# Weight splits moved from GpSimd to VectorE, and four numbers of the planner changed, in a hybrid attention layer

## The chip, the cores and the metric

One Trainium2 chip, one core. The metric is device microseconds of one execution; the time of a kernel is the median of its runs. Engines are named as in the profile: PE is TensorE (PEld its weight load, which overlaps it), DVE VectorE, ACT ScalarE, POOL GpSimd, SP the engine that issues most transfers.

## What is computed

One decoder layer on 2048 tokens of width 1024, float32:

```
h = rms_norm(x)
c_q, c_kv, k_rope, gdn_qkv, gdn_a, gdn_b, mem_q, gate = split(h @ w_in)
o_mla = causal softmax attention, 4 heads, q and k from low-rank c_q, c_kv, with rotary parts
o_gdn = gated delta rule in chunks, 4 heads:
    T = (strict_lower(k_beta k^T * decay) + I)^-1         # one triangular system per chunk
    v_new = u - w @ state;  o = q e^g @ state + a @ v_new  # state carried from chunk to chunk
o_mem = softmax attention over 256 memory tokens, 4 heads, k and v = rms_norm(mem) @ w_mem_kv
x = x + concat(o_mla, o_gdn, o_mem) * silu(gate) @ w_out
return rms_norm(x)
```

## The kernel before, in words

All large products run on PE in a float32 form of reduced width. To keep precision each operand is split into a high part (a rounded copy) and a low part (the rest), and a product is three matmuls: high by high, high by low, low by high (`mm3`).

Three stages follow each other. **The input projection** takes the tokens in two halves (`hf`) of two blocks of 512 tokens (`b`), and streams the columns of `w_in` as units: a unit is half the depth of 128 columns, one load `wr` of 256 KB, one split into `wh` (copy on ACT, sometimes DVE) and `wl` (subtraction, `w_split`, L614), and 24 matmuls `ip`. Beside it run the background jobs: the delta-rule heads (`delta_head`), the low-rank products (`low_rank`, with `q_use` and `kv_use`, matmuls `qb`, `kb`, `vb`) and the projection of the memory tokens (`mem_proj`, matmuls `mk` and `mv`); their weights are loaded as `bw` and split into `bwh` and `bwl` in `small_weights` (L1100). **Attention** has the matmuls `sc` (scores), `pt` (transposes of the probabilities) and `av` (values). **The output projection** has `op`.

For a delta-rule head, rows of decays and norms go to memory and come back broadcast over the partitions (`gr`, `fr`); there are two loads of `gr`, one for each block, and the second is issued after the first block's last product `kk` (L929). The triangular systems of a head are solved on POOL: the matrices go out (`lsys`), come in as `lt` (L944), 62 POOL instructions on `pr` and `X` solve them, the result goes out (`tsys`) and in (`inv`), and DVE transposes and PE matmuls `inv` build the larger inverse (L966 and below). The scan over the chunks (`pa`, `r`, `vn`, `st`) follows.

The order of the work is set by **a planner in the kernel's own Python**. It keeps a clock for each engine (`T`), adds a modelled cost for each instruction (`pool_cost` L223 for POOL, `pool_dma` L284 for its transfers), and after each group of PE work (`pump`) resumes the background jobs whose time has come: `yield n` in a job asks for at least n ns on PE's clock before its next step. The framework's scheduler may still move an instruction within its queue. Every operation is recorded at one line (L259), SP's transfers at L305, POOL's at L294. `lesser(name)` (L628) chooses POOL for a subtraction when the modelled POOL is free and no solve is near (`solving`), DVE otherwise.

A tile's buffer comes from a ring with a fixed number of places; a new tile waits until the instructions that read the old one in its place are done. `wr` has two places, so that the load of a unit waits for the `wl` of the unit two before it. Scores `s` and the solver's `lt` are in one ring (`page`).

Of the kernel before, what the change touches and what calls it, by code (L numbers as in the profile page):

```python
# [67 lines left out]
def hybrid_layer(ctx, tc, a, out):  # L68
# [84 lines left out]
    in_psum = set()  # L153
    tiles = set()
    step_end = [0.0]
    solving = [0.0]
    tab = [None]

    def free(ap):
        return int(np.prod(ap.shape[1:]))  # L160
# [61 lines left out]

    def pool_cost(op, args, kw, out):  # L223
        if op == "tensor_tensor":
            return 147 + 2.1 * free(out)
        fast = op == "tensor_scalar" and kw["op0"] == ALU.mult and kw.get("op1") == ALU.add
        return 160 + (0.85 if fast or op == "memset" else 3.4) * free(out)

# [55 lines left out]
    def pool_dma(out, in_):  # L284

        touch(in_, out)
        t = max(T["POOL"], T["PE"], arrival(in_, "POOL"), used.get(out.tensor.name, 0.0),
                floor.get(out.tensor.name, 0.0)) + 600
        T["POOL"] = t
        t += 1500 + free(out) * out.shape[0] * 4 / 200  # L290
        wrote(out, "SP", t + 1000)
        step_end[0] = max(step_end[0], t + 1000)
        used[in_.tensor.name] = max(used.get(in_.tensor.name, 0.0), t + 200)
        pinned(nc.gpsimd.dma_start(out=raw(out), in_=raw(in_)))  # L294
# [319 lines left out]
    def w_split(w):  # L614
        wh = sb.tile([P, 512], F32R, name="wh", tag="wh", bufs=3)
        copy(wh, w)
        wl = sb.tile([P, 512], F32R, name="wl", tag="wl", bufs=3)
        lesser("wl").tensor_tensor(wl, w, wh, op=ALU.subtract)
        return wh, wl

    def copy(out, in_):
# [5 lines left out]

    def lesser(name):  # L628

        return G if max(T["POOL"], solving[0]) <= T["PE"] + SLACK[name] else V  # L630

    class Job:

# [209 lines left out]
    def delta_head(hf, h, q, k, res):  # L843
# [52 lines left out]
        for b in range(2):  # L896
            bs = slice(b * 512, (b + 1) * 512)
            nq, nb, ne = (t.rearrange("p (c t) -> p c t", t=P) for t in cur)

            gc = cols[:, 0, h * 8 + b * 4:h * 8 + b * 4 + 4]  # L900
            gr3 = gr.rearrange("p (c t) -> p c t", t=P)
            V.tensor_tensor(gr3, gr3, gc.unsqueeze(2).broadcast_to([P, 4, P]), op=ALU.subtract)
            V.tensor_tensor(gr3, gr3, neg.unsqueeze(1).broadcast_to([P, 4, P]), op=ALU.add)
            A.activation(gr, gr, AF.Exp)
            k3, q3 = (t[:, bs].rearrange("p (c t) -> p c t", t=P) for t in (k, q))
            V.tensor_tensor(kq[:, :, 0, :], k3, nb, op=ALU.mult)
            yield 0
            V.tensor_tensor(kq[:, :, 1, :], q3, nq, op=ALU.mult)
            V.tensor_tensor(q3, q3, ne, op=ALU.mult)
            V.tensor_tensor(gr3, gr3, nk[:, b * 4:b * 4 + 4].unsqueeze(2).broadcast_to([P, 4, P]), op=ALU.mult)  # L910
            yield 0
            if b == 0:
                cur = rows(1)
                yield SPARE
            for c2 in range(2):
                ps = psg("kk")
                for c in range(2):
                    cc = c2 * 2 + c
                    PE.matmul(ps[:, c * 256:(c + 1) * 256], k[:, b * 512 + cc * P:b * 512 + (cc + 1) * P],
                              kq[:, cc, :, :], start=True, stop=True)  # L920
                o = b * 4 + c2 * 2
                ps4 = ps.rearrange("p (c i t) -> p c i t", c=2, i=2)
                dec = gr3[:, c2 * 2:c2 * 2 + 2, :]
                V.tensor_tensor(LT[:, o:o + 2, :], ps4[:, :, 0, :], dec, op=ALU.mult)
                atm = sb.tile([P, 2, P], F32, name="atm", tag="atm", bufs=2)
                V.tensor_tensor(atm, ps4[:, :, 1, :], dec, op=ALU.mult)
                dma(out=at_d[hf][h][:, o * P:(o + 2) * P], in_=atm.rearrange("p c t -> p (c t)"), awaited=False)
                if b == 0 and c2 == 1:
                    gr = decay_row(1)  # L929
                yield 0  # L930
        give(A=1)
        done["rows"] = done.get("rows", 0) + 1
        for bk in range(4):
# [8 lines left out]
        pool_dma(out=X, in_=a["eye4"])  # L942
        for cs in range(4):
            pool_dma(out=lt[cs * 32:(cs + 1) * 32].rearrange("p j i -> p (j i)"), in_=lsys[hf][h])  # L944
        solving[0] = T["POOL"] + 25000
        yield 2000
        pr = sb.tile([P, 80], F32, name="pr", tag="pr", bufs=1)
        for j in range(31):
# [5 lines left out]
            G.tensor_tensor(X[:, 0:n, j + 1:32], X[:, 0:n, j + 1:32], prv, op=ALU.subtract)  # L954
        for cs in range(4):
            pool_dma(out=tsys[hf][h].rearrange("s (n e) i -> e s n i", e=4)[cs], in_=X[cs * 32:(cs + 1) * 32])
        solving[0] = T["POOL"] + 12000
        yield from take(TT=1)
        yield 0
        give(lt=1)  # L960
# [8 lines left out]
        for n in (32, 64):  # L969
            pairs = [(2 * n * p, slice(2 * n * p, 2 * n * p + n), slice(2 * n * p + n, 2 * n * p + 2 * n))  # L970
                     for p in range(64 // n)]
            mid = t2("mid", (P, 8 * n))
            mid3 = mid.rearrange("p (c t) -> p c t", t=n)

            def sl(c):
                return slice(c * n, (c + 1) * n)
            for o, lo, hi in pairs:
                for i in range(n // 32):
                    for j in range(i, n // 32):
                        src, dst = slice(o + i * 32, o + i * 32 + 32), slice(o + j * 32, o + j * 32 + 32)  # L980
                        V.transpose(mid3[dst, :, i * 32:i * 32 + 32], TT[src, :, dst])
                        if i < j:
                            G.memset(mid3[src, :, j * 32:j * 32 + 32], 0.0)
            yield 0
            ps = psg("inv")
            for c in range(NCK):
                for o, lo, hi in pairs:
                    PE.matmul(ps[hi, sl(c)], LT[lo, c, hi], mid[lo, sl(c)], start=True, stop=True)
            for o, lo, hi in pairs:
                if o:  # L990
                    A.activation(mid[hi, :], ps[hi, 0:8 * n], AF.Copy, scale=-1.0)
                else:
                    V.tensor_scalar(mid[hi, :], ps[hi, 0:8 * n], -1.0, None, op0=ALU.mult)
            yield 0
            ps = psg("inv")
            for c in range(NCK):
                for o, lo, hi in pairs:
                    PE.matmul(ps[lo, sl(c)], mid[hi, sl(c)], TT[hi, c, hi], start=True, stop=True)
            for o, lo, hi in pairs:
                (A.copy if o else V.tensor_copy)(TT[lo, :, hi], ps[lo, 0:8 * n].rearrange("p (c t) -> p c t", t=n))  # L1000
            yield 0
# [89 lines left out]
    def small_weights(srcs):  # L1091
# [6 lines left out]
        def split(w):  # L1098
# [1 line left out]
            wh = sb.tile([P, n], F32R, name="bwh", tag="m2", bufs=9)  # L1100
            copy(wh, w)
            wl = sb.tile([P, n], F32R, name="bwl", tag="m2", bufs=9)
            lesser("bwl").tensor_tensor(wl, w, wh, op=ALU.subtract)
            return wh, wl
        w = load(srcs[0])
        yield 2800
# [50 lines left out]
    def q_use():  # L1157
# [9 lines left out]
        def use(hf, t, hs, ls, wh, wl):  # L1167
# [10 lines left out]
            for b in range(2):  # L1178
# [1 line left out]
                cs, sn = t2("cs"), t2("sn")  # L1180
                trig_load(cs, 0, hf * 2 + b, 4)
                trig_load(sn, 1, hf * 2 + b, 4)
                yield 2000
                r1, r2 = project(b, hs, ls, *half), project(b, hs, ls, wh, wl)
                tA, tB, tC = t2("ra"), t2("rb"), t2("rc")
                V.tensor_tensor(tA, r1, cs, op=ALU.mult)
# [1010 lines left out]
```

## Time and profile before

| what | us |
|---|---|
| median of 3 runs (1814.57 to 1819.68) | 1818.56 |
| the profiled execution, its own time | 1822.34 |
| its span on the core | 1820.6 |
| PE busy in the span | 1746.9 (96%) |
| DVE busy | 1158.6 (64%) |
| POOL busy | 500.4 (27%) |

The span is the time from the first to the last instruction on the core. Busy times overlap between engines. An engine's idle time is put down to what ended it. The granted clock of TensorE is 1.00 at 2.4 GHz and 0.50 at 1.2 GHz, so that a stretch's mean between these tells how much of it ran at the lower level. The projection ends near 1110 us, attention near 1550 us.

### The profile page before, as it was taken

Reading aid. Unit: us, or ns where it says so; the run is one execution under the profiler, and the core shown is the slowest. Engines: PE = TensorE matmul, PEld = TensorE weight load, DVE = VectorE, ACT = ScalarE, POOL = GpSimd, SP = SyncE. Lnnn points to the kernel's source line nnn. Section 1 sums busy time; section 2 is a strip of 40 time slices with the busy share of each in tenths; the row PEclk is TensorE's granted clock in tenths of the full one; section 3 lists DMA queues with packets and bytes.
Section 4 is the critical chain, followed back from the end, with each engine's and each line's share of the span. In section 5 each row is a group of like instructions: output and inputs, shape, how many; then the busy total and the mean of one; then the engine's idle time right before and its main releaser. Section 6 shows DMA issues by size and latency. Waiting matters only on the chain.

```text
span 1820.6 us, 28632 instructions
## 1 busy us (share of the span) xinstructions
PE 1746.9 (96%) x9776; PEld 1471.2 (81%) x9776; DVE 1158.6 (64%) x2622; ACT 734.6 (40%) x1884; POOL 500.4 (27%) x894
## 2 busy tenths in 40 slices
PE   7999999999999999899999997999999999999998
PEld 5778788888777777788888876899999998888886
DVE  6777766786785858445566653777676778345443
ACT  6444233342442535213453423455455556222121
POOL 1422752443521124352112625001111012412120
PEclk9999999999999999999999998999999999999999
DMA  7544474456555344564555479145252527566551
GB/s 265 163 128 150 137 237 137 131 160 211 154 170 176 121 147 116 184 194 138 182 199 176 141 216 265 61 127 178 70 177 71 159 88 224 167 195 199 168 162 53
DMA packets 225826, 291.19 MB, mean 160 GB/s; under 512 B 30320, under 2 KB 130672, under 8 KB 225680
## 3 DMA queue, kind: packets, MB, share of 16 engines
q1 hardware_dynamic: 218640, 273.62, 48.3%
q0 software_dynamic: 7040, 15.74, 3.0%
q8 instruction: 77, 1.26, 0.3%
q14 instruction: 69, 0.57, 0.1%
HBM read 197.79 MB, written 91.49 MB: 159 GB/s over the span
## 4 chain that ended last, share of the span: by engine, by line
PE 54%; DMA 4%; DVE 3%; POOL 1%; issue 1%; ACT 1%; SPq 1%; DVEq 0%; ACTq 0%; POOLq 0%
PE op L259 14%; PE ip L259 13%; PE sc L259 9%; PE av L259 7%; PE pt L259 4%; PE pa L259 2%; PE qb L259 1%; PE inv L259 1%; DVE y L259 1%; PE kk L259 1%; DMA craw<-craw 1%; SPq L305 1%; PE kb L259 1%; PE mk L259 1%; POOL X L259 1%
## 5 line engine op out<-in xcount | busy, mean ns | idle before, releaser
L259 PE MATMUL ip<-hh,wh 128*128 128x512 f32 x1088 | 459.8, 423 | 12.6 <-ACT hh L259 9.1
L259 PE MATMUL ip<-hh,wl 128*128 128x512 f32 x1088 | 433.8, 399 | 5.1 <-DVE wl L259 4.0
L259 PE MATMUL ip<-hl,wh 128*128 128x512 f32 x1088 | 432.3, 397 | 0.0
L259 POOL TENSOR_TENSOR wl<-wr,wh 128x512 fp32r<-128x512 f32 x84 | 120.2, 1431 | 493.9 <-ACT wh L259 403.9
L259 PEld LDWEIGHTS ip<-hh,wl 128*128 128x128 f32 x1088 | 208.3, 191 | 52.7 <-DVE wl L259 4.5
L259 PEld LDWEIGHTS ip<-hh,wh 128*128 128x128 f32 x1088 | 209.1, 192 | 49.5 <-ACT hh L259 9.1
L259 PEld LDWEIGHTS ip<-hl,wh 128*128 128x128 f32 x1088 | 209.2, 192 | 35.4 <-DVE hl L259 0.5
L259 ACT CAST wh<-wr 128x512 fp32r<-128x512 f32 x144 | 88.9, 618 | 148.6 <-PE ip L259 99.1
L259 DVE TENSOR_TENSOR tl<-pt,th 128x512 fp32r<-128x512 f32 (+2 forms) x208 | 119.8, 585 | 32.6 <-ACT th L259 30.2
L259 PE MATMUL av<-th,vn 128*128 128x256 f32 x576 | 133.2, 290 | 1.9 <-ACT th L259 1.9
L259 PE MATMUL sc<-kn,qn 128*128 128x512 f32 (+2 forms) x480 | 134.0, 379 | 0.0
L259 PE MATMUL op<-wop,mh 128*128 128x512 f32 x416 | 130.6, 394 | 0.0
L259 DVE SCALAR_TENSOR_TENSOR y<-raw,gdn_conv,y 128x512 f32<-128x512 f32 x144 | 116.5, 814 | 16.1 <-ACT y L259 14.7
L259 ACT CAST th<-pt 128x512 fp32r<-128x512 f32 (+2 forms) x160 | 80.6, 512 | 105.6 <-PE pt L259 98.7
L259 POOL TENSOR_TENSOR pr<-X,lt 128x60 f32<-128x60 f32 (+24 forms) x248 | 92.4, 373 | 49.2 <-DMA lt<-lsys 30.3
L259 PEld LDWEIGHTS av<-th,vn 128*128 128x128 f32 x576 | 99.2, 189 | 6.8 <-ACT th L259 3.0
L259 POOL TENSOR_TENSOR X<-X,pr 128x60 f32<-128x60 f32 (+24 forms) x248 | 95.9, 386 | 19.4
L294 POOL DMA_DIRECT2D mix<-mo x64 | 34.8, 544 | 226.5 <-ACT mo L259 186.8
L259 PE MATMUL sc<-kr,qr 128*128 128x512 f32 (+2 forms) x320 | 96.7, 380 | 0.0
L259 ACT ACTIVATE s<-s,m 128x768 f32<-128x768 f32 (+13 forms) x71 | 79.0, 1114 | 41.7 <-DVE mx L259 35.2
L259 PEld LDWEIGHTS op<-wop,mh 128*128 128x128 f32 x416 | 77.4, 188 | 17.5
L259 PE MATMUL pt<-ident,s 128*128 128x128 f32 x544 | 84.2, 276 | 6.2 <-DVE vt L259 6.0
(285 smaller groups left out, 3522.5 us busy)
## 6 DMA issues: line engine op xcount, KB each, us to landing
wr<-in_w_in SPq DMA_DIRECT2D x148, 256.0 KB
fr<-rows_n SPq DMA_DIRECT2D x48, 256.0 KB
mxo<-mix SPq DMA_DIRECT2D x16, 768.0 KB
craw<-craw SPq DMA_DIRECT2D x40, 256.0 KB
x<-in_xT SPq DMA_DIRECT2D x32, 256.0 KB
gatem<-gt SPq DMA_DIRECT2D x32, 256.0 KB
qn<-qn SPq DMA_DIRECT2D x32, 256.0 KB
vn<-v SPq DMA_DIRECT2D x32, 256.0 KB
```

Source lines behind the costliest of these rows:

```text
L259: return pinned(f(*args, **kw))
L294: pinned(nc.gpsimd.dma_start(out=raw(out), in_=raw(in_)))
L305: ins = pinned(nc.sync.dma_start(out=raw(out), in_=raw(in_)))
```

## The change

Five things. The subtraction of every weight split goes to VectorE, in `w_split` and in `small_weights`; only the opening's own split still asks `lesser`. With that `solving` falls away. The planner's POOL costs rise: a `tensor_tensor` from 147 + 2.1 n to 290 + 2.25 n ns, a POOL transfer's fixed part from 1500 to 2500 ns. The job waits 2500 ns in place of 0 after issuing the second `gr`, and 5000 in place of 2000 after issuing the loads of the sine and cosine tables (`cs`, `sn`) in `q_use`. In the inverse, two steps wait `SPARE` (700 ns) in place of 0.

```
     def pool_cost(op, args, kw, out):
         if op == "tensor_tensor":
-            return 147 + 2.1 * free(out)
+            return 290 + 2.25 * free(out)
...
-        t += 1500 + free(out) * out.shape[0] * 4 / 200
+        t += 2500 + free(out) * out.shape[0] * 4 / 200
...
-        lesser("wl").tensor_tensor(wl, w, wh, op=ALU.subtract)
+        V.tensor_tensor(wl, w, wh, op=ALU.subtract)
         return wh, wl
...
-        return G if max(T["POOL"], solving[0]) <= T["PE"] + SLACK[name] else V
+        return G if T["POOL"] <= T["PE"] + SLACK[name] else V
...
                 if b == 0 and c2 == 1:
                     gr = decay_row(1)
-                yield 0
+                    yield 2500
+                else:
+                    yield 0
...
-        solving[0] = T["POOL"] + 25000
...
-        solving[0] = T["POOL"] + 12000
...
-            yield 0
+            yield SPARE
             ps = psg("inv")
...
-            yield 0
+            yield SPARE
             ps = psg("inv")
...
-            lesser("bwl").tensor_tensor(wl, w, wh, op=ALU.subtract)
+            V.tensor_tensor(wl, w, wh, op=ALU.subtract)
...
                 trig_load(sn, 1, hf * 2 + b, 4)
-                yield 2000
+                yield 5000
                 r1, r2 = project(b, hs, ls, *half), project(b, hs, ls, wh, wl)
```

Since the planner's clocks move, nearly everything in the projection stands in another order. Three places.

VectorE, second half of the tokens, third head, before: the two blocks' decay rows are `gr_9573` and `gr_9854`, and `LT` and `atm` are the evacuations of the first block's products `kk`.

```order
L259 TENSOR_TENSOR LT_9572<-kk_9828,gr_9573 128x256
L259 TENSOR_TENSOR atm_9832<-kk_9828,gr_9573 128x256
L259 TENSOR_SCALAR nt_9881<-ro_9838 128x8
L259 TENSOR_SCALAR nt_9881<-nt_9881 128x8
L259 TENSOR_SCALAR ro_9838<-ro_9838 128x8
L259 TENSOR_TENSOR gr_9854<-gr_9854,cols_6560 128x512
L259 TENSOR_TENSOR mhl_9798<-mx_9800,mhl_9796 128x512
L259 TENSOR_TENSOR LT_9572<-kk_9848,gr_9573 128x256
L259 TENSOR_TENSOR atm_9852<-kk_9848,gr_9573 128x256
```

And now, where the rows are `gr_9579` and `gr_9823`:

```order
L258 TENSOR_TENSOR LT_9578<-kk_9816,gr_9579 128x256
L258 CAST rc_9762<-rc_9762 128x2
L258 TENSOR_TENSOR atm_9820<-kk_9816,gr_9579 128x256
L258 TENSOR_TENSOR rc_9762<-rc_9762 128x2
L258 SCALAR_TENSOR_TENSOR y_9740<-raw_9796,gdn_conv_247,y_9740 128x512
L258 SCALAR_TENSOR_TENSOR y_9740<-raw_9741,y_9740 128x512
L258 SCALAR_TENSOR_TENSOR y_9740<-raw_9796,gdn_conv_247,y_9740 128x512
L258 SCALAR_TENSOR_TENSOR gg_9808<-oT_9836,gdn_norm_245,gg_9808 128x512
L258 SCALAR_TENSOR_TENSOR y_9740<-raw_9796,gdn_conv_247,y_9740 128x512
L258 TENSOR_TENSOR dg_9846<-ident_227,rc_9762 128x256
L258 TENSOR_TENSOR dg_9848<-ident_227,rc_9762 128x256
L258 TENSOR_TENSOR gr_9823<-gr_9823,cols_6027 128x512
```

The first instruction on the second row stood ahead of the first block's last evacuation; now it stands eight instructions behind it.

PE in the projection of the memory tokens, before:

```order
L259 MATMUL mk<-mhl,bwh 128x256 x2
L259 MATMUL mk<-mhl,bwl 128x256
L259 MATMUL ip<-hh,wh 128x512
L259 MATMUL ip<-hl,wh 128x512
L259 MATMUL ip<-hh,wl 128x512
L259 MATMUL mk<-mhl,bwh 128x256 x2
```

And now (`tr` are transposes, `pa` the scan's products):

```order
L258 MATMUL mk<-mhl,bwl 128x256
L258 MATMUL pa<-st_odd,y 128x128
L258 MATMUL pa<-vn,aT 128x128
L258 MATMUL tr<-ident,gv 128x128 x4
L258 MATMUL tr<-ident,y 128x128 x4
L258 MATMUL mk<-mhl,bwh 128x256 x2
L258 MATMUL pa<-st_254,y 128x128
L258 MATMUL mk<-mhl,bwl 128x256
```

From the first `mk` to the 48th `mv` the order had 69 `ip` matmuls between; now it has 3.

POOL around the eighth and last solve, before; `th` and `tl` are the tiles of the first attention block on the diagonal, of which POOL clears a corner.

```order
L294 DMA X<-in_eye 128x256
L259 TENSOR_TENSOR wl<-wr,wh 128x512
L259 MEMSET cmask 128x512
L1334 AFFINE_SELECT cmask<-cmask 128x512
L259 MEMSET mid 32x8x32
L259 TENSOR_TENSOR wl<-wr,wh 128x512 x2
L294 DMA lt<-lsys_3_104 32x1024 x4
L259 MEMSET th 128x128
L259 MEMSET tl 128x128
L259 TENSOR_TENSOR pr<-X,lt 128x31
```

And now, from the solve's end:

```order
L258 TENSOR_TENSOR X<-X,pr 128x8
L293 DMA tsys_3_112<-X 256x1x32 x4
L258 MEMSET th 128x128
L293 DMA inv_280<-tsys_3_112 32x8x32
L258 MEMSET tl 128x128
L293 DMA inv_280<-tsys_3_112 32x8x32 x3
L258 MEMSET mid 32x8x32
```

The subtractions are gone from the queue, and the first clearing has moved from ahead of the solve to behind it, the second half of it behind a transfer that waits for `tsys`.

## Rows read from the trace of the kernel before

**Rows 1.** Page, part 1: busy us, share of span, instructions.
```profile
PE 1746.9 (96%) x9776; PEld 1471.2 (81%) x9776; DVE 1158.6 (64%) x2622; ACT 734.6 (40%) x1884; POOL 500.4 (27%) x894
```

**Rows 2.** Waits of PE: who waited for whom, us in total, times, longest.
```profile
PE ip L259 <- POOL wl L259: 1.0, 3, 0.4
```

**Rows 3.** Stretches: length, busy us of PE PEld DVE ACT POOL, clock, DMA share, GB/s.
```profile
30.00:75.00 45.00, 38.51 (x153) 29.40 (x152) 38.07 (x94) 26.63 (x53) 12.07 (x12) 0.93 0.70 202
540.00:570.00 30.00, 26.73 (x128) 21.67 (x127) 16.91 (x35) 9.01 (x20) 5.90 (x4) 0.95 0.68 221
745.00:770.00 25.00, 19.62 (x103) 15.77 (x102) 9.48 (x18) 4.17 (x8) 4.51 (x7) 0.86 0.52 167
1084.80:1141.40 56.60, 47.01 (x262) 38.66 (x260) 23.53 (x80) 15.10 (x48) 25.74 (x79) 0.85 0.86 240
```

**Rows 4.** Timeline, 562 to 568 us: start, length, operation, [idle before and its end].
```profile
562.55 0.69 DVE L259 TENSOR_TENSOR ra<-qb,cs 128x512 f32<-128x512 f32 x1 [6.57 <-DMA cs<-trig]
...
567.15 0.80 PE L259 MATMUL pa<-st,y 128*128 128x128 f32 x2 [2.39 <-DVE st_odd L259]
```

**Rows 5.** Timeline, 752 to 763 us.
```profile
752.43 1.31 POOL L259 TENSOR_TENSOR wl<-wr,wh 128x512 fp32r<-128x512 f32 x1
...
754.67 0.38 SPq L305 DMA_DIRECT2D gr<-rows_g  x1
...
759.62 0.69 DVE L259 TENSOR_TENSOR gr<-gr,cols 128x512 f32<-128x512 f32 x1 [8.60 <-DMA aT<-at]
...
762.12 1.07 PE L259 MATMUL inv<-mid,LT 32*32 32x32 f32 x20 [5.28 <-DVE mid L259]
```

**Rows 6.** Waits of SP's queue: us in total, times, longest.
```profile
SPq L305 <- POOL wl L259: 182.8, 59, 11.7
```

**Rows 7.** Timeline of PE and DVE, 312 to 316 us.
```profile
312.11 0.48 PE L259 MATMUL ip<-hh,wh 128*128 128x512 f32 x1
312.43 0.39 PE L259 MATMUL ip<-hl,wh 128*128 128x512 f32 x1
312.66 0.39 PE L259 MATMUL ip<-hh,wl 128*128 128x512 f32 x1
...
313.53 0.69 DVE L259 TENSOR_TENSOR gr<-gr,cols 128x512 f32<-128x512 f32 x1 [4.04 <-DMA gr<-rows_g]
...
315.26 0.49 PE L259 MATMUL pa<-st_odd,y 128*128 128x128 f32 x2 [1.97 <-DVE st L259]
```

**Rows 8.** Timeline, 1085 to 1142 us: the last solve and the entry into attention.
```profile
1085.23 0.42 DVE L259 TENSOR_TENSOR LT<-kk,gr 128x256 f32<-128x256 f32 x1 [0.34 <-PE kk L259]
...
1127.78 2.32 POOL L294 DMA_DIRECT2D tsys<-X  x4 [0.34 <-POOL X L259]
...
1135.34 2.33 POOL L294 DMA_DIRECT2D inv<-tsys  x4 [5.25 <-DMA tsys<-X]
...
1141.39 0.39 PE L259 MATMUL av<-th,vn 128*128 128x256 f32 x1
```

**Rows 9.** Instructions on tiles wl, y: count, ns least/median/most, starts; last, mean of the y.
```profile
L259 POOL TENSOR_TENSOR wl<-wr,wh x84: 1266/1293/4325, 32.7 to 1081.7; 128x512 fp32r<-128x512 f32 x84
L259 DVE TENSOR_TENSOR wl<-wr,wh x64: 673/686/1192, 35.8 to 1107.5; 128x512 fp32r<-128x512 f32 x64
L259 DVE SCALAR_TENSOR_TENSOR y<-raw,gdn_conv,y x144: 729/751/1785, 80.5 to 1079.2; 128x512 f32<-128x512 f32 x144
L259 DVE SCALAR_TENSOR_TENSOR y<-raw,gdn_conv,y 128x512 f32<-128x512 f32 x144 | 116.5, 814 | 16.1 <-ACT y L259 14.7
```

**Rows 10.** Timeline, 1039 to 1044 us: a memory weight's load and split, two products.
```profile
1039.47 0.33 SPq L305 DMA_DIRECT2D bw<-in_w_mv  x1
...
1043.57 0.62 ACT L259 CAST bwh<-bw 128x512 fp32r<-128x512 f32 x1 [3.17 <-DMA bw<-in_w_mv]
1043.72 0.28 PE L259 MATMUL mv<-bwh,mhl 128*128 128x256 f32 x1
1043.84 0.28 PE L259 MATMUL mv<-bwl,mhl 128*128 128x256 f32 x1
```

More of the change, by code (lines that the diff above doesn't have):

```diff
@@ L155, in hybrid_layer @@
     step_end = [0.0]
-    solving = [0.0]
     tab = [None]
```

## The prediction, on record before the run

> **What bounds the kernel now.** I read five views in this order. The page's first part gives the engines: PE is busy for 1746.9 of the span's 1820.6 us, DVE for 1158.6, POOL for 500.4 [rows 1]. So PE is the bound on average, and about 74 us is all that its waits cost. The waits of PE then ask whether the instructions that move are what PE waits for. They are not: the 84 subtractions on POOL held PE three times, for 1.0 us together [rows 2]. What they hold is SP's queue, 182.8 us in 59 waits [rows 6], because a new `wr` needs the place that `wl` still reads. The stretches show where PE is idle and what else that costs: the granted clock is 0.85 to 0.95 in stretches in which PE waited, so part of them ran at 1.2 instead of 2.4 GHz [rows 3]. The timelines give what ended last at each stall [rows 4, 5, 7, 8]. The tiles give the prices [rows 9]. So a gain is counted as idle time plus what the lower level cost.
>
> The sum is made against the profiled execution, 1822.3 us (span 1820.6 and 1.7 around it), which lies 3.8 above the median of the three runs. A change of this kernel under 0.3%, 5.5 us, can't be told from none.
>
> **Part 1: the subtractions.** POOL loses 84 `wl` at a median of 1.293 us, DVE gains them at 0.686: 57.6 us [rows 9]. The order moves 11 `bwl` too, none wider than a `wl`, so at most 7.5 more: DVE's added work is 58 to 65 us. None of it is on PE by itself; DVE has 1820.6 − 1158.6 = 662 us idle.
>
> Some of it comes back. DVE's `wl` take 0.686 at the median but up to 1.192, the `y` 0.751 but up to 1.785 [rows 9], and the slow ones that I looked at stand beside a POOL subtraction. The mean of the 144 `y` is 814 ns against the median of 751: 144 × 0.063 = 9 us in this group alone. The `y` are 116.5 of DVE's 1158.6 us; the same share, 9 / 116.5, on half of DVE's 1158.6 us would be 45; if only the `y` suffer, 9. I take 25, between the two, so DVE's net load is +33 to +40. The Trainium skill ("Perfetto Trace Analysis", "Optimizing Scalar/DVE Operations") advises to offload work from a saturated DVE, even to GPSIMD, which speaks against this change wherever DVE is full. It adds that the two share a read port of SBUF, so that an offload between them may not help, and the slowed `y` agree with that half. By the first half the next two places only lose, by the second nothing is lost; the sum goes by the rows.
>
> *Where DVE is dense it costs.* (a) The opening, 30 to 75 us: DVE is busy 38.07 of 45 us, PE 38.51 [rows 3]. Six or seven of the moved `wl` lie there in the order, 4.5 us against 6.9 of DVE's idle. Bounds: 0 if they fit, 5 if PE pays all; PE already idles 6.5 us there, so I take **+3**.
>
> (b) The memory tokens. The planner, with other POOL costs, now runs `mk` and `mv` late and almost without `ip` between (order above). From the first `mk` to the 48th `mv` PE has 144 of them at 0.12 us, the spacing of two starts [rows 10], 17.3 us, plus some 60 small ones at about that, 7.3, plus 13 changes of form at 0.09 (below): 26 us. DVE has in that stretch 37 operations of 512 wide at 0.69, 8 of 256 to 384 at 0.42 [rows 8], and 26 narrower, which I put at 5 us together: 25.5 + 3.4 + 5 = 34. So DVE ends some 8 us later than PE could; it starts with a lead, which I put at 3. That leaves 5 of idle and, by the stretches, 2 of clock: **+7**. Lower bound 0, if the lead is larger. Upper bound: a memory weight needs 1043.57 − 1039.47 = 4.1 us from issue to its copy [rows 10]; if 12 of the 16 came one after the other like that, 49 us, 23 idle, with clock 29.
>
> (c) Elsewhere DVE is later by 3% (33 to 40 us in the 1110 of the projection) at the places where PE already waits for it, 1.97 to 2.39 us at a time [rows 4, 7]. Bounds −4 (two such stalls go, relieved by the contention) and +6 (three more come); I take **+3**, since a load that is certain stands against a relief that is an estimate.
>
> *What it saves on PE.* After a product of another form an `ip` takes 0.32 us from start to start, then 0.23 [rows 7]: a change costs 0.09. In the order PE returns to `ip` from other forms 507 times instead of 535: 28 × 0.09 = **−2.5**. Bounds 0 and −2.5.
>
> **Part 2: tables, `yield 5000`.** At 562.55 DVE had waited 6.57 us for `cs`, and PE then 2.39 at 567.15, because the scan's `st_odd` stands behind on DVE [rows 4]. With 3 us more between load and use, and a queue of SP that no longer waits on POOL, 2.4 goes; the clock of 540 to 570 was 0.95 [rows 3], worth 0.05 × 30 = 1.5. **−3.9**; bounds 0 (the wait only becomes another tile's) and −3.9.
>
> **Part 3: the second row, `yield 2500`, and `SPARE`.** At 752.43 a `wl` runs on POOL; behind its end SP issues `gr`, at 754.67; DVE waits for it 8.60 us, until 759.62, and `mid` with it, so that PE stands 5.28 us before `inv` at 762.12 [rows 5]. Both are met: the `wl` is not on POOL, and the job gives the row 2.5 us more, so that the first block's evacuations stand ahead of it (order above; so in 6 of the 8 heads, before in 3). Idle 5.3 and clock 0.14 × 25 = 3.5 [rows 3]: **−8.8**, bounds −4 (half of a stall that returns at the next row) and −8.8. The same wait of 4.04 on DVE at 313.53 cost PE 1.97 [rows 7], and there is one more like it; two heads keep the old order, so I take half of about 3.2: **−1.6**, bounds 0 and −3.2. SPARE moves only which matmuls stand between the steps of the inverse: 0, covered by the `ip` that are there; without these it is part of the case below.
>
> **Part 4: the entry into attention.** From the last `kk` to the first `av`, 56.6 us, PE was busy 47.0 at clock 0.85 [rows 3]; its matmuls at their spacing (0.23 for 512 wide, 0.12 for 256 [rows 7, 10], others in proportion, and 18 changes of form) are 35.5, so the stretch loses 21. Now `th` and `tl` are cleared behind the solve (third place above). In the last solve `tsys` went out 42.55 us after `LT` and took 2.32, then `inv` waited 5.25 [rows 8]. So the first `av` can't come before 42.55 + 2.32 = 44.9 us after `LT` (for `th`), and 44.9 + 5.25 = 50.1 for `tl`. PE has 32.6 us of matmuls to that point: a loss of 12.3 to 17.5, against 21. The gain is 8.7 to 3.5; since `av` needs both tiles I take **−4.5**. Lower bound of the gain 0, if the solve ends later; upper 11.5, if POOL, without subtractions, is 3 us faster.
>
> **The sum.** −2.5 − 3.9 − 8.8 − 1.6 − 4.5 = −21.3; +3 + 7 + 3 = +13. Net −8.3: 1814.0 for an execution like the profiled one, 1810.3 for the median; I say **1810**.
>
> **The rivals.**
> *B, all of it hidden.* DVE's load is paid by the contention that goes, and (a), (b), (c) cost nothing: −21.3, 1797. For it: POOL's subtractions are the only thing that SP's queue waits on so long [rows 6], and the slowest `y` [rows 9]. Against: (b) has DVE work of 34 us in 26 of PE's, and no contention to take away is in that count.
>
> *C, slower: the memory weights pace PE.* One mechanism, one place: with the `ip` gone from between the `mk` and `mv`, each weight's chain (load, copy, subtraction on DVE, products) stands bare. At 4.1 us for each of 12 weights the stretch costs 29 instead of 7: +13.7 net, 1832. The gain is gone when all costs reach 21.3, and the kernel is slower beyond what can't be told from none when this stretch alone costs some 21: 16 idle and 5 clock, weights 3.5 us apart. For it: 3.17 us of ACT's wait for a load even with `ip` about [rows 10], and a job that works two weights ahead at most. Against: loads two ahead overlap, which halves 4.1.
>
> *D, no change: stalls are dealt anew.* The planner's clocks move everything, each stall that goes is replaced by one that the trace of before can't show (`SPARE`'s steps without `ip`, another row, another page): 1814 to 1821, say 1818. For it: PE's 74 us are spread over many places, 2 to 5 us each where I looked [rows 4, 5, 7]. Against: the longest of them, at 762 us, has a cause that the order removes [rows 5]. That the change doesn't do what it says is ruled out by the order.
>
> **How the numbers follow.** Forecast 0.36, B 0.22, D 0.20, C 0.22. The forecast's own range is 1803 to 1819 (its bounded terms, not all at one end): 0.28 faster, 0.08 within 0.3%. B is faster. D gives 0.13 same, 0.03 faster, 0.04 slower. C is slower. Together 0.53, 0.21, 0.26. The range, 1795 to 1829, leaves out the better half of B and the worse half of C, 0.2 together.
>
> **What would show it.** POOL's `wl` fall to those of the opening, and DVE has about 33 to 40 us more busy time, less if contention was larger. The `y` should come to 0.75 at the mean. No wait over 3 us of DVE for `cs` or `gr` where PE follows; clock near 1.00 there. Between the first `mk` and the last `mv`: 33 us; 45 or more is C. From the last `LT` to the first `av`: 45 to 50. The prediction is wrong if that memory stretch loses over 20 us, if the time falls while DVE's busy time rises by 60 or more, or if PE's idle time is the same at other places.

## The result, and the profile after

The change is slower. The median of 7 runs is 1833.61 us (1826.92 to 1840.10), of the kernel before 1818.77 in 7; the ratio is 1.0079, with a 95% interval from 1.0054 to 1.0104. The profiled execution took 1835.48 us, span 1833.7: 13 us more than before's.

The changed kernel's page, part 1, against [rows 1]:

```profile
PE 1745.5 (95%) x9776; PEld 1468.7 (80%) x9776; DVE 1180.0 (64%) x2714; ACT 742.8 (41%) x1889; POOL 367.6 (20%) x799
```

POOL lost 132.8 us and DVE gained only 21.4, where 95 moved subtractions add 58 to 65. PE has the same 9776 matmuls and waits longer. The changed kernel's waits of PE (who waited for whom, us in total, times, longest):

```profile
PE av L258 <- DVE th L258: 16.0, 1, 16.0
PE ip L258 <- DVE wl L258: 8.4, 4, 4.0
PE rn L258 <- DVE fac L258: 8.3, 1, 8.3
...
PE mv L258 <- ACT bwh L258: 5.9, 6, 1.9
...
PE mk L258 <- ACT bwh L258: 3.6, 4, 1.7
```

Stretches of the changed kernel (length, then busy us and instructions of PE, PEld, DVE, ACT, POOL, granted clock, DMA share, GB/s): the first lies where one of [rows 3] lay, the second holds the second row of the same head, the third has the last `kk` at its start and the first `av` at its end; the fourth runs from the first `mk` to the 48th `mv`, the last three are wide.

```profile
540.00:570.00 30.00, 29.93 (x152) 24.58 (x151) 21.89 (x61) 12.42 (x29) 0.00 (x0) 1.00 0.33 111
755.00:790.00 35.00, 35.00 (x158) 29.05 (x157) 25.44 (x42) 16.99 (x42) 0.00 (x0) 1.00 0.42 142
...
1085.70:1142.40 56.70, 37.74 (x207) 29.90 (x205) 23.51 (x57) 12.18 (x29) 26.80 (x77) 0.89 0.92 256
...
1015.60:1061.60 46.00, 37.52 (x239) 31.94 (x237) 31.01 (x68) 19.42 (x70) 30.09 (x71) 0.93 0.59 169
...
0.00:150.00 150.00, 124.76 (x515) 99.70 (x516) 108.93 (x242) 78.53 (x169) 15.73 (x22) 0.93 0.56 172
500.00:1000.00 500.00, 485.61 (x2571) 400.38 (x2572) 326.73 (x697) 200.70 (x527) 67.46 (x160) 0.99 0.51 168
1000.00:1250.00 250.00, 215.94 (x1456) 184.81 (x1457) 156.75 (x426) 101.50 (x293) 67.82 (x177) 0.95 0.55 158
```

The stretch from the first `mk` to the 48th `mv` before, and the same wide stretches:

```profile
1011.60:1047.20 35.60, 35.10 (x231) 31.81 (x230) 21.38 (x44) 18.31 (x60) 27.95 (x66) 1.00 0.50 143
...
0.00:150.00 150.00, 130.13 (x537) 103.68 (x538) 111.14 (x232) 75.85 (x168) 41.51 (x38) 0.95 0.60 185
500.00:1000.00 500.00, 476.95 (x2456) 391.93 (x2457) 310.49 (x638) 193.79 (x530) 134.39 (x207) 0.98 0.51 164
1000.00:1250.00 250.00, 234.27 (x1552) 203.62 (x1551) 155.70 (x416) 104.19 (x289) 73.91 (x183) 0.95 0.57 166
```

Where the change aimed, it hit, but not without new stalls. The stretch of the second row has PE full and the clock at 1.00. The first row above is of other work than in [rows 3], since the tables are now used at 664.88; there DVE waits for PE and no longer for the load. Two waits of PE of over 4 us, both in the scan of a head, stand ahead of it:

```profile
618.55 0.80 PE L258 MATMUL pa<-st_odd,y 128*128 128x128 f32 x2 [4.13 <-DVE st L258]
...
657.01 0.80 PE L258 MATMUL pa<-vn,kt 128*128 128x128 f32 x2 [4.33 <-ACT vn L258]
...
664.88 0.69 DVE L258 TENSOR_TENSOR ra<-qb,cs 128x512 f32<-128x512 f32 x1 [2.84 <-PE qb L258]
```

In all, PE was busy 8.7 us more of the stretch from 500 to 1000 us. It was busy 5.4 us less of the opening and 18.3 less of the stretch from 1000 to 1250 us, at a clock no higher. Two places show how. The changed kernel's timeline at the entry into attention (start, length, operation, idle before and its end):

```profile
1125.48 2.31 POOL L293 DMA_DIRECT2D tsys<-X  x4 [0.33 <-POOL X L258]
1127.69 0.31 POOL L258 MEMSET th<- 128x128 f32 x1
1133.65 0.60 POOL L293 DMA_DIRECT2D inv<-tsys  x1 [5.64 <-DMA tsys<-X]
1134.23 0.23 POOL L258 MEMSET tl<- 128x128 f32 x1
...
1140.05 0.43 DVE L258 STREAM_TRANSPOSE mid<-inv 32x256 f32<-32x256 f32 x1 [15.32 <-DMA inv<-tsys]
...
1141.89 0.42 DVE L258 CAST th<-pt 128x256 fp32r<-128x256 f32 x1
...
1142.37 0.58 PE L258 MATMUL av<-th,vn 128*128 128x256 f32 x1 [16.01 <-DVE th L258]
```

The clearings were done by 1134.5, but on DVE a transpose of the eighth inverse stands ahead of `th`, and waits for the whole solve. In the memory stretch the weights' copies on ACT (count, ns least, median, most, first and last start) stand with few products between:

```profile
L258 ACT CAST bwh<-bw x15: 601/617/631, 1016.4 to 1073.3; 128x512 fp32r<-128x512 f32 x15
```

That is (1073.3 − 1016.4) / 14 = 4.1 us from copy to copy. Between them PE had three `ip` and the small products of a delta-rule head, and was busy 37.5 of 46.0 us. Before, ten copies of these weights (1013.06 to 1047.96) stood 3.9 us apart, hardly closer, but with 69 `ip` between PE was busy 35.1 of 35.6 us.

### The profile page after: what moved, and what is told of

Same layout as the page of the kernel before. It is cut to its first block, busy times and chain, and to the rows that moved or that the text cites. A ratio compares the mean times of both kernels' runs of the same rounds, so it can differ in the third digit from the quotient of the medians.

```text
span 1833.7 us, 28548 instructions
## 1 busy us (share of the span) xinstructions
PE 1745.5 (95%) x9776; PEld 1468.7 (80%) x9776; DVE 1180.0 (64%) x2714; ACT 742.8 (41%) x1889; POOL 367.6 (20%) x799
## 4 chain that ended last, share of the span: by engine, by line
PE 74%; DMA 10%; DVE 6%; ACT 4%; issue 2%; POOL 1%; SPq 1%; DVEq 0%; ACTq 0%; POOLq 0%
PE ip L258 30%; PE op L258 12%; PE sc L258 10%; PE av L258 7%; PE pt L258 4%; PE pa L258 3%; PE qb L258 2%; PE inv L258 1%; DMA sn<-trig 1%; PE kk L258 1%; DMA gr<-rows_g 1%; SPq L304 1%; DMA bw<-in_w_q_b 1%; DMA wr<-in_w_in 1%; DMA mxo<-mix 1%
## 5 line engine op out<-in xcount | busy, mean ns | idle before, releaser
L258 PE MATMUL ip<-hh,wh 128*128 128x512 f32 x1088 | 452.8, 416 | 11.9 <-ACT hh L258 8.2
L258 DVE TENSOR_TENSOR wl<-wr,wh 128x512 fp32r<-128x512 f32 x148 | 102.9, 697 | 66.6 <-ACT wh L258 64.0
L293 POOL DMA_DIRECT2D lt<-lsys x32 | 16.0, 504 | 637.0 <-DMA lsys<-LT 343.8
L258 DVE SCALAR_TENSOR_TENSOR y<-raw,gdn_conv,y 128x512 f32<-128x512 f32 x144 | 106.4, 748 | 15.5 <-ACT y L258 14.4
L258 PEld LDWEIGHTS sc<-kn,qn 128*128 128x128 f32 x480 | 81.0, 190 | 8.2
```

What stands on the lines that cost most here:

```text
L258: return pinned(f(*args, **kw))
```

## The experiments

The two theories at the start: **D**, VectorE's added work makes PE wait; **R**, the engine is harmless, and what costs is the new order that the planner deals when its numbers change. All ratios are to the kernel before, with their 95% intervals. The kernel before ran again beside each group of runs (medians from 1815.2 to 1817.4 us), so differences between runs of different groups are read from the ratios; 0.001 is 1.8 us.

**The swap alone.** The planner keeps every number and booking of before; where it picks POOL, the instruction goes on VectorE's queue.

```
+    def shadow(name, out, w, wh):
+        if lesser(name) is V:
+            V.tensor_tensor(out, w, wh, op=ALU.subtract)
+        else:
+            note("POOL", pool_cost("tensor_tensor", (), {}, out), [out], [w, wh])
+            pinned(nc.vector.tensor_tensor(out, w, wh, op=ALU.subtract))
...
-        lesser("wl").tensor_tensor(wl, w, wh, op=ALU.subtract)
+        shadow("wl", wl, w, wh)
...
-            lesser("bwl").tensor_tensor(wl, w, wh, op=ALU.subtract)
+            shadow("bwl", wl, w, wh)
```

> Before's planner with all its numbers and decisions; only where it chose POOL for a wl or bwl the instruction is put on VectorE (the planner still books it on POOL). Theory R (the change lost by the new order that its planner numbers deal, the engine is harmless): 1805 to 1822 us, DVE busy about 1180, the y near 0.75 us at the mean. Theory D (VectorE's 58 to 65 us of added work make PE wait): 1828 or more, with PE's waits on DVE wl and on the scan's tiles up by 10 us or more.

1803.5 us, ratio 0.9928 (0.9902 to 0.9953): faster by 13 us. D falls. The swap's page, part 1, and its group of the `y`, against the last of [rows 9]:

```profile
PE 1739.1 (97%) x9776; PEld 1466.5 (81%) x9776; DVE 1179.1 (65%) x2717; ACT 734.9 (41%) x1884; POOL 362.4 (20%) x799
...
L259 DVE SCALAR_TENSOR_TENSOR y<-raw,gdn_conv,y 128x512 f32<-128x512 f32 x144 | 106.8, 748 | 14.9 <-ACT y L259 13.5
```

DVE rose by 20.5 us where 58 to 65 were added. Summed over the groups of one form, the instructions other than subtractions took 30 us less, 9.5 of them in the `y`; the other 10 or so lie in records that overlap, of which busy time counts the union. That POOL's subtractions had slowed them is seen in the trace of before: the 23 of the 144 `y` that overlap one took 1146 ns at the mean, the other 121 took 751.

**The last transposes later**, in the changed kernel.

```
         yield 4000
+        if done["solves"] == 8:
+            yield 10000
```

> The changed kernel; the eighth inverse yields 10000 ns more before its transposes, so that on VectorE the first th and tl of attention stand ahead of the transposes that wait for inv<-tsys. All up to the attention's entry keeps its order. Theory H (a blocked queue: the 16.0 us that PE waited for th, with the 17 us at the lower clock behind it, come from the place of these transposes): the wait falls to 8 us or less (tl is still cleared behind the first transfer of inv on POOL) and the time to 1815 to 1825. Rival (PE has nothing else there: the solve itself ends last): the wait moves to an inv or a later av, 1829 to 1838.

1818.7 us, 1.0012 (0.9999 to 1.0025). By the ratios, 12 us of the change's time (7 to 17) come from the place of these transposes. The medians differ by 15, but in the two profiled executions, whose order is the same that far, the last `ip` starts at 1121.6 and at 1117.0, so that some 5 us between them lie ahead of the edit. What is left is the predicted wait for `tl`'s clearing; the run's timeline:

```profile
1127.44 0.60 POOL L293 DMA_DIRECT2D inv<-tsys  x1 [5.58 <-DMA tsys<-X]
1128.02 0.23 POOL L258 MEMSET tl<- 128x128 f32 x1
...
1128.30 0.58 PE L258 MATMUL av<-tl,vn 128*128 128x256 f32 x1 [4.77 <-POOL tl L258]
```

**Old POOL numbers, and no new yields**, each in the changed kernel.

```
-            return 290 + 2.25 * free(out)
+            return 147 + 2.1 * free(out)
...
-        t += 2500 + free(out) * out.shape[0] * 4 / 200
+        t += 1500 + free(out) * out.shape[0] * 4 / 200
```

> The changed kernel with the planner's old POOL numbers (147 + 2.1 n, 1500); subtractions on VectorE and all new yields stay. Theory P (the truer POOL costs push every solve and head later in the plan, pages are held longer, and the memory weights and the last solve end up bare): 1805 to 1822, the stretch of mk and mv loses under 8 us and no wait for th over 5 us at attention's entry. Rival Y (the yields do that): 1828 to 1840, both losses stay.

1842.9 us, 1.0146 (1.0112 to 1.0180). Slower still, and outside both expected ranges: theory P falls. The memory stretch now had 120 `ip` between, but the last `kk` came at 1109.3 us, behind the last `ip` at 1084.0. So a kernel with that stretch mended can be slow by a late last head.

```
-                    yield 2500
-                else:
-                    yield 0
+                yield 0
...
-            yield SPARE
+            yield 0
...
-                yield 5000
+                yield 2000
```

> The changed kernel without its new yields (0 after the second gr, 2000 behind the tables, 0 in the inverse); subtractions on VectorE and the new POOL numbers stay. Theory P: 1828 to 1842, the stretch of mk and mv stays without ip and loses 14 us or more, and DVE's waits for cs and for the second gr come back. Rival Y: 1805 to 1822.

1828.4 us, 1.0065 (1.0041 to 1.0090), which can't be told from the change. Rival Y falls too. This is the other way to be slow: the last `kk` came early, but from the first `mk` to the 48th `mv` no `ip` was left, and the stretch took 71.5 us:

```profile
L258 PE MATMUL kk<-kq,y x128: 377/379/795, 156.9 to 1072.3; 128*128 128x256 f32 x128
...
1002.10:1073.60 71.50, 48.13 (x338) 41.55 (x336) 42.18 (x90) 24.49 (x77) 32.40 (x72) 0.81 0.34 106
```

Neither new number nor yields alone explains it, so the booking of the subtractions was left. The next runs add one part at a time.

**Swap and yields; swap and POOL numbers; booked on vector.** The first two put the change's own lines, the removed ones of the two diffs above, on the swap. The last is the engine's part of the change alone, on the kernel before:

```
-        return G if max(T["POOL"], solving[0]) <= T["PE"] + SLACK[name] else V
+        return G if T["POOL"] <= T["PE"] + SLACK[name] else V
...
-        lesser("wl").tensor_tensor(wl, w, wh, op=ALU.subtract)
+        V.tensor_tensor(wl, w, wh, op=ALU.subtract)
...
-            lesser("bwl").tensor_tensor(wl, w, wh, op=ALU.subtract)
+            V.tensor_tensor(wl, w, wh, op=ALU.subtract)
```

> The swap alone plus the change's new yields (2500 after the second gr, 5000 behind the tables, 700 in the inverse), planner's POOL numbers and bookings as before. Theory R (any new number deals a new order, good or bad by where heads and stalls fall): its sign isn't given by what the yields are for; with the last kk behind the last of the ip as in this order (no sc between the last kk and the first av), 1808 to 1830. Rival G (the yields do what they are for, each removes its stall): 1788 to 1800.

1812.3 us, 0.9984 (0.9971 to 0.9997): the yields cost about 9 us of the swap's 13. Rival G falls.

> The swap alone plus the change's POOL numbers in the planner (290 + 2.25 n, 2500), the subtractions still booked on POOL. Theory R: 1805 to 1830 by its new order, 138 ip stand between the mk and mv, so that stretch loses under 8 us. Rival N (truer numbers place instructions where they are really ready): 1788 to 1803.

1797.8 us, 0.9898 (0.9876 to 0.9919): 6 us under the swap, at the edge of the noise. It is in rival N's range and outside theory R's.

> Kernel before with the subtractions on VectorE for the planner as well; its POOL numbers and yields are the old ones. Theory K (booking them on the planner's VectorE is enough to deal the late heads): 1822 to 1845, last head's products behind the last ip. Rival (only the new numbers and yields did harm): as the swap alone, 1800 to 1808.

1838.5 us, 1.0124 (1.0099 to 1.0149): 35 us slower than the swap, which differs only in the clock on which the planner books the subtractions (`solving` decides nothing any more). Theory K holds.

**Later transposes and rope's tables**, in the changed kernel: the edit above and, in `key_rope`,

```
         trig_load(sn, 1, hf * 2 + b, 2)
-        yield 2000
+        yield 6000
```

> The changed kernel with the eighth inverse's transposes later, as in the run before, and 6000 in place of 2000 behind the tables of the key's rotary part. Theory C (memory weights cost what they do because no ip stands between): with 75 ip between the mk and mv in place of 30 and the first mk far earlier, that stretch loses under 8 us; with the rope's wait (8 to 9 us of PE for fac) gone too, 1796 to 1810. Rival (weights pace the memory products wherever they stand, and the rope's load is late at any place): 1815 or more.

1815.0 us, 0.9988 (0.9977 to 0.9999): a miss for the time, where the rival's range begins, and right for the stretch. This run's row from its first `mk` to its last `mv`:

```profile
860.70:913.60 52.90, 51.80 (x423) 46.76 (x422) 23.95 (x48) 15.99 (x39) 3.20 (x6) 1.00 0.46 140
```

With `ip` between, the same weights cost nearly nothing. The rope did not gain: PE still waited 7.2 us for `fac`. In the changed kernel the wait looks so:

```profile
103.94 0.61 SPq L304 DMA_DIRECT2D cs<-trig  x1
...
111.14 1.37 DVE L258 TENSOR_TENSOR ra<-kr,cs 32x512 f32<-32x512 f32 x2 [7.51 <-DMA cs<-trig]
...
119.11 0.37 PE L258 MATMUL rn<-ident,fac 128*24 128x128 f32 x1 [8.26 <-DVE fac L258]
```

Issue to use is 7.2 us, and behind `ra` on DVE stood the chain that ends in `fac`.

**Booked nowhere**, on booked on vector, and the same edit on the whole change.

```
+    def shadow(out, w, wh):
+        t = max(T["PE"], arrival(w, "DVE"), arrival(wh, "DVE"), floor.get(out.tensor.name, 0.0)) + 603
...
+        wrote(out, "DVE", t)
+        pinned(nc.vector.tensor_tensor(out, w, wh, op=ALU.subtract))
```

> As booked on vector, but the planner books the subtraction on no engine: it is ready 603 ns after its inputs and VectorE's clock in the planner doesn't move. On the chip it runs on VectorE like the others. Theory K (the 60 us that the planner's VectorE clock gains are what deals the late heads): 1795 to 1810; the last kk stands ahead of the last ip again. Rival L (what does harm is that POOL's clock in the planner is freed of its 84 subtractions): 1828 or more, like booked on vector.

1803.8 us, 0.9937 (0.9915 to 0.9959). L falls: POOL's planner clock is as free here as in booked on vector. The edit also frees VectorE's planner clock of the 64 `wl` that the planner of before had booked there itself; the swap keeps these bookings and is as fast.

> The changed kernel with all its parts, but its subtractions booked on no engine in the planner. Theory K: the second half's first head is picked ahead of the low-rank query weights again, mk and mv have 105 ip between (30 in the change), and the time falls by 15 us or more: 1798 to 1818. Rival L: 1828 to 1840.

1809.4 us, 0.9960 (0.9945 to 0.9974): the whole change, with that one booking out, is faster than before, and 22 us faster than as it was (24 by the medians). L falls here too. The memory stretch has its `ip` again and PE full:

```profile
969.80:1010.30 40.50, 40.39 (x250) 36.20 (x249) 23.84 (x42) 13.87 (x30) 1.99 (x4) 1.00 0.61 186
```

**Picks of booked**: the swap, with `pick` taking the units in the order of booked on vector (`turn` is that list).

```
+        for seq in js:
+            if seq[0].m == turn[0] and seq[0].ready():
+                turn.pop(0)
...
+        return None
```

> The swap alone with the planner's bookings of before, but the units of the projection picked in the order that booked on vector picked them (the second half's first head behind the query's low-rank products). Theory O (the order of the units is how the booking does harm): 1822 to 1842. Rival M (it is the place of each instruction beside the units, not the units' order): 1800 to 1812.

1820.0 us, 1.0018 (1.0000 to 1.0036), between the two expected ranges: the units' order alone costs 16 us of the 35.

**Another deal**, on the swap alone.

```
-LAT = 150
+LAT = 170
```

> The swap alone with another number of the planner that stands for nothing on the chip: the slack behind each step (LAT) 170 ns in place of 150. The order of the units stays. Theory R: a new deal with the same units moves the time by 8 us at most either way from the swap alone, 1796 to 1812. Rival (any new deal is worth as much as the differences found so far): outside of that.

1803.6 us, 0.9926 (0.9900 to 0.9953): no difference. This one deal that keeps the units' order is worth nothing. One deal can't bound the scatter of all, but the runs together speak against scatter: without the hand-made moves (the later transposes, the forced picks), the five kernels that book these subtractions in VectorE's turn take 1827.0 to 1842.9 us, the seven that book them elsewhere or not at all 1791.7 to 1812.3.

**Booked in its turn, at 0 ns**, on booked nowhere.

```
-        t = max(T["PE"], arrival(w, "DVE"), arrival(wh, "DVE"), floor.get(out.tensor.name, 0.0)) + 603
+        t = max(T["DVE"], T["PE"], arrival(w, "DVE"), arrival(wh, "DVE"), floor.get(out.tensor.name, 0.0))
+        T["DVE"] = t
```

> As booked on vector, but the planner books each subtraction on VectorE at 0 ns: it takes its turn there (VectorE's planner clock goes to the time at which the weight's copy is ready) and adds no work. Theory K1 (the added 60 us of work in the planner's clock deal the late heads): 1798 to 1812. Theory K2 (the turn does: the clock runs ahead to the arrival of a weight, and every step of the heads behind it is planned later): 1822 to 1842.

1827.0 us, 1.0064 (1.0046 to 1.0083): 23 of the 35 us without any work in the planner's clock. K2 is the larger part, the work the smaller.

**Booked, with the first picks**: booked on vector, with the same edit of `pick` and the list of booked nowhere.

> Booked on vector, with the units picked in the order that booked nowhere picked them; where the buffers are not free in the plan, the planner waits for them. Theory O (half of the booking's 35 us is the order of the units): 1815 to 1825. Rival (the planner's steps beside the units are late all the same, and holding the order only moves the gap): 1830 to 1850.

1832.7 us, 1.0086 (1.0056 to 1.0116): 6 us back where theory O had 14 to 23, and that within the noise. The rival holds: with the order held the heads were late all the same, the last `kk` at 1097.9.

**Booked nowhere, with the POOL numbers** (290 + 2.25 n and 2500, as in the change).

> Booked nowhere plus the change's POOL numbers, without its yields; also the change without yields and without its bookings. If the parts add up (swap -13, booking 0, POOL numbers -6): 1792 to 1804, as fast as the swap with the POOL numbers or faster. If the parts do not add (each deal by itself): up to 1815.

1791.7 us, 0.9861 (0.9827 to 0.9895): 25 us faster than before and the fastest here, and clear of booked nowhere (0.9937), so that here the POOL numbers give 12 to 14. It is also the change without its yields and bookings, so that against the change booked nowhere (0.9960) the yields cost 18 us in this deal.

Which way most of these runs went is seen in one row, the products `kk` of all heads (first and last start): the change, booked on vector, the swap alone, booked nowhere with the POOL numbers, and the change booked nowhere.

```profile
L258 PE MATMUL kk<-kq,y x128: 377/379/483, 159.3 to 1085.7; 128*128 128x256 f32 x128
```
```profile
L258 PE MATMUL kk<-kq,y x128: 377/379/483, 157.8 to 1110.9; 128*128 128x256 f32 x128
```
```profile
L259 PE MATMUL kk<-kq,y x128: 377/379/632, 146.4 to 1066.8; 128*128 128x256 f32 x128
```
```profile
L258 PE MATMUL kk<-kq,y x128: 377/379/483, 144.9 to 1065.1; 128*128 128x256 f32 x128
```
```profile
L258 PE MATMUL kk<-kq,y x128: 377/378/795, 146.9 to 1087.4; 128*128 128x256 f32 x128
```

The last head's solve and scan follow its last `kk`. At 1065 to 1067 us there is projection left to hide them; at 1087 to 1111 there is little or none. The row alone does not decide: the change without its yields had its last `kk` at 1072.3 and was slow by the memory stretch, and the change booked nowhere had it at 1087.4 and was fast. The change itself is slow by the memory stretch and the entry, not by that row: its last `kk` is where before's was (1085.7 and 1084.8), but in the order 103 `ip` stand between the last `kk` and the first `av` (63 before), while the memory weights had three and the transposes held up DVE.

Wide stretch, booked on vector, and then booked nowhere with the POOL numbers: PE's time and clock behind late and early heads.

```profile
1000.00:1250.00 250.00, 221.71 (x1400) 186.69 (x1400) 142.37 (x380) 96.09 (x277) 67.66 (x177) 0.90 0.49 150
```
```profile
1000.00:1250.00 250.00, 233.14 (x1587) 202.77 (x1586) 159.15 (x460) 109.15 (x304) 68.79 (x190) 0.97 0.56 162
```

## Why the prediction was wrong

**The step that failed** is the one that costed part 1 by VectorE's load on the chip: "DVE's net load is +33 to +40", with +3 for the opening, +7 for the memory stretch and +3 "elsewhere". On the chip the load cost nothing: the swap alone gained 13 us, and the net was +20.5, where I took 25 as returned and some 40 were. What did cost came by the new order, and the two terms for it were mis-sized:
- The memory stretch, +7, was priced as DVE's 34 us of work against PE's 26. DVE was busy only 31.0 of the 46.0 us; the weights, one load after the other, set the pace. Counted as the prediction counts, a stretch's length less its matmuls at their spacing (0.23 us for 512 columns, 0.12 for 256, in the traces 0.11 for 128 and 0.22 for `kk`), it lost 17.8 us, and the same stretch before lost 1.4: +16 in place of +7.
- The entry, −4.5, followed POOL's queue only. From the last `kk` to the first `av` PE lost 22.5 us by the same count, before 19.7: +3 in place of −4.5. There DVE's transposes of the eighth inverse stood ahead of `th` and waited for the solve.

These two make 17 of the 21 us between the forecast's −8.3 and the +13 of the profiled executions. By the same count the stretch from 150 to 1000 us gained 12, not far from what parts 2 and 3 said.

The prediction read the new order from three places and took it as given; it did not ask which of the diff's parts dealt it. The runs name it: the planner's clock of VectorE. A weight is split ahead of its use, and its booking moves that clock to the time when the weight's copy will be ready; every later step of the heads on VectorE is then planned behind it. Booked on POOL, as 95 of them were, the same jump stood on a clock that the heads need mainly for their solves. Taking the booking off gives 35 us in one kernel and 22 to 24 in the change; the jump without work costs 23.

**Point by point.**
- Tables, −3.9, and second row, −8.8: the stalls of [rows 4, 5] went, the second with clock 1.00 in its stretch; near the tables two others came (4.1 and 4.3 us), which is rival D's mechanism. But the parts made for this, the yields, cost 9 us on the swap and 18 on booked nowhere with the POOL numbers. The terms were about right where they stood and wrong as gains of the yields: these also make the heads longer (last `kk` at 1087.4 against 1065.1), and that comes back at the end.
- Rows −1.6 and changes of form −2.5: too small to be seen; PE's busy time fell by 1.4. The count of the changes was off: in the two traces PE returns to `ip` from other products 345 times before and 297 now, not 535 and 507.
- Opening, +3: PE's busy time in the first 150 us fell by 5.4 us. The largest wait there, 8.3 for `fac`, is no `wl` but a table's load ahead of the chain on DVE, and before's PE had no such wait. Waits for `wl` were the smaller part: 6.5 us in the first 160 us, before 4.6.
- Memory stretch, +7: 46.0 us from the first `mk` to the 48th `mv`, where I had 33 and called 45 rival C. Rival C was right in this place, weights 4.1 us apart; the term should have been 16, below C's 29 and near the 21 that C needed to show. I had argued against C that loads two ahead overlap. They hardly did: three `mv` weights of the changed kernel were issued at 1042.36, 1047.13 and 1049.94 and copied at 1046.74, 1051.65 and 1056.75. The trace of before had the pace already, ten copies 3.9 us apart.
- Entry, −4.5: the row's bound, 50 us from the last `LT` to the first `av`, held as a bound, but it came to 56, as long as before. I had followed POOL's queue and not DVE's, where the transposes stood ahead of `th`.
- `y` back to 0.75 us: 0.748. POOL's subtractions off SP's queue: they were, and DVE's took their place in it. To the 182.8 us in [rows 6] belong 81.5 that SP waited for DVE's `wl` before, 264.3 in 92 waits together; now it is 213.6 in 86.

SP's waits for DVE's `wl`, before and in the changed kernel (us, times, longest):

```profile
SPq L305 <- DVE wl L259: 81.5, 33, 8.5
...
SPq L304 <- DVE wl L258: 213.6, 86, 12.4
```

The measured time, 1833.6, is near rival C's 1832, but in part by luck: C's mechanism is there at about half of C's price, and the entry, which was not on the list, gave the rest. As to the Trainium skill ("Perfetto Trace Analysis", "Optimizing Scalar/DVE Operations"): the swap agrees with its second half, that an offload between the two might not help: of the 58 to 65 us added, DVE's busy time kept 20.5. Its first half, on a saturated DVE, does not bind here, where DVE is 65% busy.

**What stays open.** Which steps of the heads slip first was not followed one by one, nor why the booking ends in a bare memory stretch in one kernel and in a late last head in another. The units' order alone is worth 16 us when put on the swap, and at most 6 when put back on booked on vector, so the two causes are not simply additive. Why the yields cost 18 us in one deal and nothing that can be told in the change is only argued (there the heads were late already). The old POOL numbers in the change were slower, not faster; that the new ones help is shown there and on booked nowhere, the way is not.

## What to carry to other kernels

In a kernel whose own planner sets the order, an edit has two effects that must be tried apart: what the instruction does on its engine, and what its booking does to the plan; emit it on the new engine with the old booking, and the other way round. Book an instruction that waits for a load on a clock that nothing urgent shares, or on none: an in-order clock that runs ahead to a weight's arrival delays all that is planned behind it. Keep independent products between products whose operands come one load at a time: counted by the spacing of the matmuls, the memory stretch lost 1 us with 69 `ip` between, 18 with three and 40 with none. And when a new order is read, follow every in-order queue at the place where the next stage begins, and look for what stands ahead of its first instruction.

## What the runs showed of the hardware

An element-wise instruction on POOL is not free for VectorE: 95 subtractions that POOL ran in some 130 us cost VectorE only 20.5 us more when it ran them itself, the `y` falling from 814 to 748 ns at the mean; before, a `y` that overlapped such a subtraction took 1146 ns, one that did not 751. And a table of half a weight's size, read once for each of two groups of partitions, took 7.2 us from issue to use in the opening; a memory weight took 4.1 in [rows 10]. What makes the difference was not tried.
